# A fused encoder layer: 20 of its 24 token-tile transposes leave TensorE for VectorE blocks of 32 and a turn through DRAM

## Chip, cores and metric

The kernel runs on one core of one Trainium2 chip. The metric is device microseconds of one execution, median of the runs: 2145.7 us before (3 runs, 2145.51 to 2145.97).

## The reference

One encoder layer for two sequences, `x_prompt` (1024 tokens, below "the long sequence") and `x_sample` (512 tokens), each with 1024 features, in float32. Cut to what matters here:

```python
xn = _rmsnorm(x, norm_mix_g)
x  = x + _token_mixer(xn, w_in, ...)       # z = xn @ w_in, two attentions, gates, @ w_out
hn = _rmsnorm(x, norm_mlp_g)
x  = x + jnp.square(jax.nn.relu(hn @ w_up)) @ w_down
y  = _rmsnorm(x, norm_final_g)
```

Both `xn @ w_in` and `hn @ w_up` contract over the 1024 features, so on TensorE the normed activations must stand with features on the partitions: a normed tile of 128 tokens by 1024 features has to be turned into eight pieces of 128 features by 128 tokens.

## The kernel before, in words

All matmuls are in float32 by three products: each operand is split into a part `h` that ScalarE (ACT) copies out rounded, and a part `l`, the rest, that VectorE (DVE) subtracts; lines 195, 196 and 197 are the products h·h, l·h and h·l. So a turned tile is needed as `xs_…h` and `xs_…l` (for the token mixer) or as pieces of seven operands `B0`…`B6` (for the MLP, which is a seven-product scheme over two blocks of 768 tokens; `pair_t` makes the operands from two tiles, j and j+3 of a block, with sums and differences `ta1`…`ta4`).

The program is one long sequence. Trunk 0 mixes the 512 tokens of `x_sample` (4 tiles), trunk 1 the 1024 tokens of `x_prompt` (8 tiles), then comes the MLP over all 12 tiles. Every engine has its own instruction queue, filled in an order that a list scheduler fixed when the program was built, and each queue runs in that order: an instruction that waits holds up all behind it on its engine. SP (SyncE) only issues transfers, POOL (GpSimd) issues some too.

- **The switch from trunk 0 to trunk 1.** The last loop of a trunk is its out-projection, tile by tile (`ops` on TensorE, added to the residual `xrs` by DVE into `hs`). In trunk 0's second half of it, the normed MLP input `xnhs` of each tile is made and stored by POOL to a DRAM tensor `hnd` (L1215). Beside it, tiles 0 to 3 of the long sequence (`xas`, loaded at L1173) are normed into `xnns` and turned by `transpose_tile` (L282): eight TensorE transposes into PSUM `ptxs` (L290), an ACT copy to `xs_0h` (L300), a DVE subtraction to `xs_0l` (L306). Three are turned there, the fourth is carried into trunk 1, whose first loop multiplies tile by tile (`zs`, `zvs`) while it norms (`xts` to `xns`, L277) and turns tiles 4 to 7 the same way (into `xs_1h`, `xs_1l`). The norm's last step needs `rs_…`, a power that POOL works out (L180).
- **The end of trunk 1.** The same out-projection stores `xnhs` of trunk 1's first four tiles to `hnd`; its other four tiles are only added to `hd` (a DRAM tensor with the residual stream) and normed later, during the MLP (`late_norm`, store at L1558). SP fetches back the tiles of the first MLP block (`hn<-hnd`, L1099), and `pair_t` runs three times, each time with 16 TensorE transposes (L330) into PSUM `pt`, ACT copies to the operands (L339) and DVE differences (L342 to L358). Behind that SP loads `rawu`, the up weights, from which DVE makes the operands `A`; then TensorE starts the MLP's products `ua`, `ub`, `uc`, `ud`.
- **The second MLP block.** `hn_load` (L1277) fetches its six tiles from `hnd` and `pair_t` runs three times more, amid the last products of block one.

Of 24 transposed tiles the trace shows 12 at L290 (four of them `x_sample`'s) and 12 in pairs at L330. The buffers that matter: normed tiles and some `xrs` tiles share a pool tag `k4` of four buffers, fetched `hn` tiles share three.

Of the kernel before, what the change touches and what calls it, by code (L numbers as in the profile page):

```python
# [61 lines left out]
def encoder(ctx: ExitStack, tc: tile.TileContext, xs, outs, w):  # L62
# [19 lines left out]
    hnd = dram.tile([NTOK, D], F32, name="hnd")  # L82
# [198 lines left out]

    def transpose_tile(xn, dest, j, nm, pin=False, between=()):  # L282
# [42 lines left out]
    def pair_t(nm, j, tiles, B, banks, tmp):  # L325

        b11, b21, b12, b22 = banks
        for halves, t in (((b11, b21), tiles[0]), ((b12, b22), tiles[1])):
            for c in range(NC8):
                nc.tensor.transpose(  # L330
                    halves[c // 4][:, (c % 4) * P : (c % 4 + 1) * P], t[:, c * P : (c + 1) * P], ident
                )
# [11 lines left out]
        y1 = tmp(f"y1{nm}")  # L344
        a2, a1, a3, a4 = (tmp(f"ta{i}{nm}") for i in (2, 1, 3, 4))
        hi(0, b11)
        nc.scalar.activation(y1, b12, AF.Copy)

# [3 lines left out]
        nc.vector.tensor_tensor(a1, y1, b11, op=ALU.subtract)  # L352
        hi(2, a1)
        nc.vector.tensor_tensor(a2, b22, a1, op=ALU.subtract)
        nc.vector.tensor_tensor(a3, b22, y1, op=ALU.subtract)
# [11 lines left out]
    class Trunk:  # L367
# [15 lines left out]
        def p0_t(self, tt, xn, between=()):  # L383
# [3 lines left out]
            transpose_tile(xn, self.xhl[tb], j, f"x{self.N}_{tt}", self.t0 + tt < 3, between)  # L387
            self.ready = max(self.ready, tt + 1)
# [7 lines left out]
    def run(tr, nxt, first):  # L396
# [100 lines left out]
        for g in range(2):  # L497
            with phase(f"phR{N}_{g}") as ph:
                xn_of, pre = {}, {}
                fresh = g == 0 and tr.ready < NT  # L500
                if fresh and not first:
# [16 lines left out]
                    xt = norm_load(x, tr.ready, ph, f"{N}_{tr.ready}")  # L518
                    xn_next = ph.tile([P, D], F32, tag="xn", name=f"xn{N}_{tr.ready}", bufs=2)
# [61 lines left out]
                def next_norm(tt):  # L581
                    xn = ph.tile([P, D], F32, tag="xn", name=f"xn{N}_{tt}", bufs=2)
                    xn_of[tt] = norm_to(xn, norm_load(x, tt, ph, f"{N}_{tt}"), gb, f"{N}_{tt}")
# [74 lines left out]
                for tt in range(NT):  # L658
                    tb, j = divmod(tt, 4)
                    nm = f"{N}_{g}_{tt}"  # L660
                    def next_tile():
                        tr.p0_t(tt + 1, xn_of.pop(tt + 1))
                        if not first and tt + 3 < NT:
                            next_norm(tt + 3)
                        elif first and tt + 2 < NT:
# [5 lines left out]
                    to_come = fresh and tr.ready <= tt + 1 < NT  # L671
# [32 lines left out]
                    if fresh and not first:  # L704
                        if tt == 0:
                            tr.p0_t(*tr.carry.pop(0))
                        if tt == 1:
                            xn_of[tr.ready] = norm_to(xn_next, xt, gb, f"{N}_{tr.ready}")
                        if tt == 2:
                            next_norm(tr.ready + 1)  # L710
# [1085 lines left out]
```

## Time and profile before

| | |
|---|---|
| median of 3 runs | 2145.7 us |
| the profiled execution's span | 2144.2 us |
| TensorE (PE) busy | 2116.2 us, 99% |
| VectorE, ScalarE, GpSimd busy | 1462.7, 1146.2, 356.1 us |
| DMA, mean over the span | 165 GB/s; queue q1 (SP's) 277927 packets, 41.9% of 16 engines |

A row of the timeline reads: start, length (both us), engine, line, operation, output<-inputs, shapes; rows that follow each other are folded as xN, and what stands in brackets is the idle time before and what ended it. `SPq` is SP issuing; a DMA's time there is that of the issue, not of the data. Groups of instructions show busy time and the mean ns of one, then the idle time of the engine just before them. Matmuls are pipelined: their lengths overlap, so what one costs is seen by when the next one starts.

### The profile page before, as it was taken

Reading aid. Unit: us, or ns where it says so; the run is one execution under the profiler, and the core shown is the slowest. Engines: PE = TensorE matmul, PEld = TensorE weight load, DVE = VectorE, ACT = ScalarE, POOL = GpSimd, SP = SyncE. Lnnn points to the kernel's source line nnn. Section 1 sums busy time; section 2 is a strip of 40 time slices with the busy share of each in tenths; the row PEclk is TensorE's granted clock in tenths of the full one; section 3 lists DMA queues with packets and bytes.
Section 4 is the critical chain, followed back from the end, with each engine's and each line's share of the span. In section 5 each row is a group of like instructions: output and inputs, shape, how many; then the busy total and the mean of one; then the engine's idle time right before and its main releaser. Section 6 shows DMA issues by size and latency. Waiting matters only on the chain.

```text
span 2144.2 us, 32083 instructions
## 1 busy us (share of the span) xinstructions
PE 2116.2 (99%) x10967; PEld 1847.3 (86%) x10967; DVE 1462.7 (68%) x2793; ACT 1146.2 (53%) x2511; POOL 356.1 (17%) x446
## 2 busy tenths in 40 slices
PE   9999999999999999999999999999999999999998
PEld 8888778888897888887888899999999988888886
DVE  6665786767657755656882877777777777659563
ACT  6664653767566644555530566566655643434342
POOL 2232310323232223333200200003000000000000
PEclk9999999999999999999999999999999999999999
DMA  6437557520122133444472665578545799688561
GB/s 190 133 98 212 152 162 251 186 71 25 57 79 68 42 95 108 131 118 112 140 240 103 213 194 184 171 248 205 165 142 157 256 353 343 212 279 281 165 206 59
DMA packets 321259, 354.08 MB, mean 165 GB/s; under 512 B 31551, under 2 KB 255431, under 8 KB 321095
## 3 DMA queue, kind: packets, MB, share of 16 engines
q1 hardware_dynamic: 277927, 279.65, 41.9%
q10 hardware_dynamic: 36016, 52.19, 7.0%
q0 software_dynamic: 7152, 20.19, 3.5%
q8 instruction: 87, 1.43, 0.3%
q14 instruction: 77, 0.63, 0.1%
HBM read 264.85 MB, written 87.88 MB: 165 GB/s over the span
## 4 chain that ended last, share of the span: by engine, by line
PE 67%; DVE 1%; issue 1%; DMA 0%; ACT 0%; POOL 0%; SPq 0%; POOLq 0%; ACTq 0%; DVEq 0%
PE dn L195 6%; PE dn L196 6%; PE dn L197 6%; PE ua L195 2%; PE ua L196 2%; PE ua L197 2%; PE ud L195 2%; PE ud L196 2%; PE ud L197 2%; PE uc L195 2%; PE uc L196 2%; PE uc L197 2%; PE gpss L195 2%; PE gpss L197 2%; PE gpss L196 2%; PE ops L197 1%
## 5 line engine op out<-in xcount | busy, mean ns | idle before, releaser
L197 PE MATMUL dn<-wd,al 128*128 128x512 f32 x624 | 242.8, 389 | 0.0
L196 PE MATMUL dn<-wd,ah 128*128 128x512 f32 x624 | 242.8, 389 | 0.0
L195 PE MATMUL dn<-wd,ah 128*128 128x512 f32 x624 | 242.7, 389 | 0.0
L1273 ACT ACTIVATE ah<-ar 128x512 fp32r<-128x512 f32 x168 | 104.4, 628 | 203.1 <-PE dn L196 177.1
L1274 DVE TENSOR_TENSOR al<-ar,ah 128x512 fp32r<-128x512 f32 x168 | 113.9, 685 | 71.6 <-ACT ah L1273 64.0
L197 PEld LDWEIGHTS dn<-wd,al 128*128 128x128 f32 x624 | 117.1, 188 | 24.4
L195 PEld LDWEIGHTS dn<-wd,ah 128*128 128x128 f32 x624 | 117.1, 188 | 24.3
L196 PEld LDWEIGHTS dn<-wd,ah 128*128 128x128 f32 x624 | 117.1, 188 | 24.2
L749 POOL TENSOR_SCALAR ps<-ps,rls 128x1024 f32<-128x1024 f32 (+1 forms) x96 | 96.8, 1010 | 225.7 <-DVE rls L748 200.4
L788 ACT ACTIVATE pths<-pTs 128x512 fp32r<-128x512 f32 x160 | 94.0, 597 | 74.0 <-PE pTs L783 71.9
L789 DVE TENSOR_TENSOR ptls<-pTs,pths 128x512 fp32r<-128x512 f32 x160 | 107.6, 686 | 37.7 <-ACT pths L788 36.9
L743 DVE TENSOR_REDUCE nms<-ss 128x1 f32<-128x1024 f32 (+1 forms) x96 | 99.8, 1040 | 25.6 <-PE ss L741 25.0
L195 PE MATMUL gpss<-xs_0h,w_gs 128*128 128x512 f32 x256 | 105.5, 412 | 0.5 <-DVE ot_Bs L440 0.4
L746 ACT ACTIVATE ps<-ss,nms 128x1024 f32<-128x1024 f32 (+1 forms) x96 | 93.2, 972 | 22.8 <-DVE nms L743 20.2
L783 PEld LDWEIGHTS pTs<-ident,ps 128*128 128x128 f32 x640 | 77.9, 140 | 28.5 <-POOL ps L749 4.3
L180 POOL TENSOR_TENSOR rs_f<-ms_f,mhalf 128x1 f32<-128x1 f32 x6 | 4.0, 667 | 590.7 <-DVE ms_f L176 590.7
L197 PE MATMUL gpss<-xs_0h,w_gs 128*128 128x512 f32 x256 | 101.1, 395 | 0.2 <-DVE w_gs L190 0.2
L196 PE MATMUL gpss<-xs_0l,w_gs 128*128 128x512 f32 x256 | 101.0, 394 | 0.0
L783 PE MATMUL pTs<-ident,ps 128*128 128x128 f32 x640 | 99.0, 274 | 1.3 <-DVE ptls L789 0.6
L1273 ACT ACTIVATE A<-S 128x512 fp32r<-128x512 f32 x128 | 75.9, 623 | 31.5 <-DVE S L1336 22.7
L957 POOL TENSOR_TENSOR bms<-rects,msks 128x384 f32<-128x384 f32 (+1 forms) x72 | 70.1, 977 | 129.1 <-DVE nmbs L974 107.6
L1392 ACT ACTIVATE c<-c 128x384 f32<-128x384 f32 x96 | 50.3, 524 | 69.4 <-DVE c L1391 69.3
(330 smaller groups left out, 6419.7 us busy)
## 6 DMA issues: line engine op xcount, KB each, us to landing
ar<-ud SPq DMA_DIRECT2D x120, 512.0 KB, 5.3
br<-in_w_mlp_down_dram SPq DMA_DIRECT2D x72, 512.0 KB, 5.2
rawu<-in_w_mlp_up_dram SPq DMA_DIRECT2D x64, 512.0 KB, 4.1
ud<-c ACTq DMA_DIRECT2D x128, 192.0 KB, 3.2
raw_gs<-in_w_in_dram SPq DMA_DIRECT2D x32, 512.0 KB, 4.0
zgs<-sgs ACTq DMA_DIRECT2D x48, 256.0 KB, 2.2
ud<-cs SPq DMA_DIRECT2D x64, 192.0 KB
raw_os<-in_w_out_dram SPq DMA_DIRECT2D x16, 512.0 KB, 3.9
```

What stands on the lines that cost most here:

```text
L195: nc.tensor.matmul(out, ah, bh, start=start, stop=False, **kw)
L196: nc.tensor.matmul(out, ah, bl, start=False, stop=False, **kw)
L197: nc.tensor.matmul(out, al, bh, start=False, stop=stop, **kw)
L743: nc.vector.tensor_reduce(nm_, s, axis=AX.X, op=ALU.max, negate=True)
L746: nc.scalar.activation(p, s, AF.Exp, bias=nm_, accum_out=l)
L749: nc.gpsimd.tensor_scalar(p, p, rl, 1.0, op0=ALU.mult, op1=ALU.mult)
L783: nc.tensor.transpose(pt[:, j * P : (j + 1) * P], PP[u, j][:, kc * P : (kc + 1) * P], ident)
L788: nc.scalar.activation(hi, pt, AF.Copy)
L789: nc.vector.tensor_tensor(lo, pt, hi.bitcast(F32), op=ALU.subtract)
L957: nc.gpsimd.tensor_tensor(bm.rearrange("p (r c) -> p r c", c=32), rects[h][:, ir : ir + kr_n, jr : jr + 32], msk[:, hf * 3 + ct, :].rearra ...
L1273: nc.scalar.activation(hi, src, AF.Copy)
L1274: nc.vector.tensor_tensor(lo, src, hi.bitcast(F32), op=ALU.subtract)
```

## The change

For trunk 1's eight tiles and the MLP's twelve, the TensorE transposes go. In their place `send_t` transposes a normed tile where it lies, in blocks of 32 by 32 (DVE, one instruction of 128x1024), and writes it to a DRAM tensor that has features as rows (`xt` for trunk 1, `hnt` in place of `hnd`) by four transfers of 32x32x32 elements, each of 1024 runs of 128 bytes: 20 transposes, 80 transfers. Trunk 1's writes are issued by SP, the MLP's by POOL. A trunk-1 tile is then fetched back by two SP transfers (128x4x128, runs of 512 bytes) straight into its `xs_…l` buffers, and `split` makes h by an ACT copy and l by a DVE subtraction in place. The MLP's tiles are fetched as before by one SP transfer each, now from `hnt` in runs of 512 bytes instead of 4 KB, and `pair_t` reads them from SBUF instead of PSUM; the copy `y1` goes, as it only kept one of its inputs out of PSUM. `x_sample`'s own four tiles are turned by TensorE as before.

```diff
+    def send_t(dst, col, t, eng):
+        v = t.rearrange("p (b i) -> p b i", i=32)
+        nc.vector.transpose(v, v)
+        rows_of = dst.rearrange("(b i) t -> i b t", i=32)
+        for a in range(4):
+            eng.dma_start(rows_of[:, :, col + 32 * a : col + 32 * a + 32], v[32 * a : 32 * a + 32])
+
+    def hn_fetch(raw, t0):
+        nc.sync.dma_start(
+            raw.rearrange("p (c t) -> p c t", t=P), hnt.rearrange("(c p) t -> p c t", p=P)[:, :, t0 : t0 + P]
+        )
...
-    def pair_t(nm, j, tiles, B, banks, tmp):
-        b11, b21, b12, b22 = banks
-        for halves, t in (((b11, b21), tiles[0]), ((b12, b22), tiles[1])):
-            for c in range(NC8):
-                nc.tensor.transpose(
-                    halves[c // 4][:, (c % 4) * P : (c % 4 + 1) * P], t[:, c * P : (c + 1) * P], ident
-                )
+    def pair_t(nm, j, tiles, B, tmp):
+        b11, b21, b12, b22 = (t[:, q * 512 : q * 512 + 512] for t in tiles for q in range(2))
...
+        def send(self, tt, xn):
...
+            send_t(self.xt, tt * P, xn, nc.sync)
+            for q in range(2):
+                nc.sync.dma_start(
+                    self.xhl[tb][1][q][:, :, js].bitcast(F32),
+                    self.xt[q * 512 : q * 512 + 512, tt * P : (tt + 1) * P].rearrange("(c p) t -> p c t", p=P),
+                )
+        def split(self, tt):
...
+            for hi, lo in parts:
+                nc.scalar.activation(hi, lo.bitcast(F32), AF.Copy)
+            for hi, lo in parts:
+                nc.vector.tensor_tensor(lo, lo.bitcast(F32), hi.bitcast(F32), op=ALU.subtract)
...
-                    xn_of[tt] = norm_to(xn, norm_load(x, tt, ph, f"{N}_{tt}"), gb, f"{N}_{tt}")
+                    tr.send(tt, norm_to(xn, norm_load(x, tt, ph, f"{N}_{tt}"), gb, f"{N}_{tt}"))
...
-                    while ahead:
-                        nxt.p0_t(*ahead.pop(0))
+                    while len(ahead) > 1:
+                        nxt.split(ahead.pop(0))
...
-                            nc.gpsimd.dma_start(hnd[rows_, :], hn)
+                            send_t(hnt, r0, hn, nc.gpsimd)
```

The order of the queues moves with it. At the switch, SP's queue stood as follows before (names end in the tile's number and a running number; `xas` and `xts` are input tiles, `raw_…` weights, `rts` rope tables):

```order
L478 DMA rawkvs1_0_4695<-in_w_in_dram 128x8x64 x2
L1173 DMA xas0_1_1_4474<-in_x_prompt_dram 128x1024
L1173 DMA xas0_1_2_4539<-in_x_prompt_dram 128x1024
L223 DMA raw_vs1_0_0_4704<-in_w_in_dram 128x4x256
L223 DMA raw_vs1_0_4_4709<-in_w_in_dram 128x4x256
L1173 DMA xas0_1_3_4600<-in_x_prompt_dram 128x1024
L223 DMA raw_gs1_2304_0_0_5390<-in_w_in_dram 128x8x128
L109 DMA gbs1_4674<-in_norm_mix_g_dram 128x1024
```

In the changed kernel the same stretch of SP's queue holds the writes (L288, into the turned tensor `xts1_4480`) and the fetches (L405) of tiles 0 to 2; those of tile 3 follow behind it, ahead of `gbs1`:

```order
L1207 DMA xas0_1_1_4490<-in_x_prompt_dram 128x1024
L288 DMA xts1_4480<-xnns0_1_0_4468 32x32x32 x4
L405 DMA xs1_0l0_4478<-xts1_4480 128x4x128
L405 DMA xs1_0l1_4479<-xts1_4480 128x4x128
L1207 DMA xas0_1_2_4549<-in_x_prompt_dram 128x1024
L223 DMA raw_vs1_0_0_4718<-in_w_in_dram 128x4x256
L223 DMA raw_vs1_0_4_4723<-in_w_in_dram 128x4x256
L223 DMA raw_gs1_2304_0_0_5391<-in_w_in_dram 128x8x128
L288 DMA xts1_4480<-xnns0_1_1_4532 32x32x32 x4
L288 DMA xts1_4480<-xnns0_1_2_4595 32x32x32
L405 DMA xs1_0l0_4478<-xts1_4480 128x4x128
L405 DMA xs1_0l1_4479<-xts1_4480 128x4x128
```

A fetch can be issued only when its tile's four writes have landed, and on SP the next tile's loads and writes stand behind it; tile 1's fetch also stands behind the first write of tile 2.

DVE's queue at the same place, before: the l part of tile 0 (`xs1_0l`, L306), the norm of tile 1 (`xnns0_1_1`), the l parts of the projection weights `wgls`, then tile 1's l part:

```order
L306 TENSOR_TENSOR xs1_0l0_4503<-ptxs1_0_4505,xs1_0h0_4501 128x4x128
L306 TENSOR_TENSOR xs1_0l1_4504<-ptxs1_0_4505,xs1_0h1_4502 128x4x128
L266 SCALAR_TENSOR_TENSOR xnns0_1_1_4529<-xas0_1_1_4474,rs_ns0_1_1_4534,gns0_4288 128x1024
L1199 TENSOR_TENSOR hs0_1_4285<-ops0_1_2_4541,xrs0_1_2_4537 128x512
L190 TENSOR_TENSOR wgls1_0_0_4682<-rawqs1_0_0_4683,wghs1_0_0_4681 128x2x256 x2
L190 TENSOR_TENSOR wgls1_0_1_4686<-rawqs1_0_1_4687,wghs1_0_1_4685 128x2x256 x2
L306 TENSOR_TENSOR xs1_0l0_4503<-ptxs1_1_4566,xs1_0h0_4501 128x4x128
```

And in the changed kernel (L418 is the l part in `split`, L285 the transpose):

```order
L285 STREAM_TRANSPOSE xnns0_1_0_4468<-xnns0_1_0_4468 128x1024
...
L418 TENSOR_TENSOR xs1_0l0_4478<-xs1_0l0_4478,xs1_0h0_4476 128x4x128
L418 TENSOR_TENSOR xs1_0l1_4479<-xs1_0l1_4479,xs1_0h1_4477 128x4x128
L190 TENSOR_TENSOR wgls1_0_0_4696<-rawqs1_0_0_4697,wghs1_0_0_4695 128x2x256 x2
...
L190 TENSOR_TENSOR wgls1_0_1_4700<-rawkvs1_0_4709,wghs1_0_1_4699 128x2x128 x2
L266 SCALAR_TENSOR_TENSOR xnns0_1_1_4532<-xas0_1_1_4490,rs_ns0_1_1_4537,gns0_4288 128x1024
L285 STREAM_TRANSPOSE xnns0_1_1_4532<-xnns0_1_1_4532 128x1024
...
L285 STREAM_TRANSPOSE xnns0_1_2_4595<-xnns0_1_2_4595 128x1024
L418 TENSOR_TENSOR xs1_0l0_4478<-xs1_0l0_4478,xs1_0h0_4476 128x4x128
```

The l part of tile 0 now stands ahead of all of `wgls` and of tile 1's norm and transpose; tile 3's norm likewise stands behind tile 2's l part, tile 4's behind tile 3's, tile 7's behind tile 5's.

At the end of trunk 1, SP's queue before, from the fetch of the second pair of MLP tiles on (`hn0_1` and `hn0_4` are that pair, `hn0_2` and `hn0_5` the third):

```order
L1099 DMA hn0_4_13264<-hnd_87 128x1024
L1166 DMA xrs1_1_4_13266<-in_x_prompt_dram 128x512
L1099 DMA hn0_2_13337<-hnd_87 128x1024
L1166 DMA xrs1_1_5_13341<-in_x_prompt_dram 128x512
L1166 DMA xrs1_1_6_13415<-in_x_prompt_dram 128x512
L1166 DMA xrs1_1_7_13444<-in_x_prompt_dram 128x512
L1099 DMA hn0_5_13339<-hnd_87 128x1024
L1309 DMA rawu0_0_0_13515<-in_w_mlp_up_dram 128x4x256
```

And now:

```order
L1200 DMA xrs1_1_4_13263<-in_x_prompt_dram 128x512
L1200 DMA xrs1_1_5_13318<-in_x_prompt_dram 128x512
L1200 DMA xrs1_1_6_13372<-in_x_prompt_dram 128x512
L1200 DMA xrs1_1_7_13401<-in_x_prompt_dram 128x512
L291 DMA hn0_4_13261<-hnt_87 128x8x128
L291 DMA hn0_2_13314<-hnt_87 128x8x128
L291 DMA hn0_5_13316<-hnt_87 128x8x128
L1339 DMA rawu0_0_0_13472<-in_w_mlp_up_dram 128x4x256
```

The four residual loads `xrs` take buffers of the tag `k4` over from normed tiles, so each waits until POOL's four writes of one tile have landed (the last of them: until POOL's addition of `xrs1_1_4` to `hd`); the fetches `hn0_4`, `hn0_2`, `hn0_5` and the weights `rawu` now all stand behind them.

63 lines of the change are left out of this document (35 added, 28 removed).

## The prediction, on record before the changed kernel ran

> **What bounds the kernel.** First the head of the page, with the engines' busy time, and the chain that ended last:
>
> ```profile
> span 2144.2 us, 32083 instructions
> ...
> PE 2116.2 (99%) x10967; PEld 1847.3 (86%) x10967; DVE 1462.7 (68%) x2793; ACT 1146.2 (53%) x2511; POOL 356.1 (17%) x446
> ...
> PE 67%; DVE 1%; issue 1%; DMA 0%; ACT 0%; POOL 0%; SPq 0%; POOLq 0%; ACTq 0%; DVEq 0%
> ```
>
> TensorE sets the end: all its idle time is 2144.2 − 2116.2 = 28 us. A transpose taken off TensorE therefore counts in full, as long as its replacement arrives in time; and whatever makes TensorE wait counts in full too. The profiled execution's span is 1.5 us under the median of 2145.7; I sum against the span and add 1.5.
>
> **What is removed.** A transpose's own length (273 ns) overlaps its neighbours', so I read its price from the starts, in the timeline of TensorE, once at L290 and once at L330:
>
> ```profile
> 368.58 1.03 PE L290 MATMUL ptxs<-ident,xnns 128*128 128x128 f32 x8
> 369.37 0.47 PE L197 MATMUL ops<-wh_os,mgs 128*128 128x512 f32 x1
> ...
> 1177.08 1.91 PE L330 MATMUL pt<-ident,hn 128*128 128x128 f32 x16
> 1178.75 0.48 PE L195 MATMUL ops<-wh_os,mgs 128*128 128x512 f32 x1
> ```
>
> Eight cost 369.37 − 368.58 = 0.79 us, sixteen 1.67 us. Eight groups of eight and six of sixteen: 8 × 0.79 + 6 × 1.67 = 16.3 us. That is all that can be gained; 160 × 273 ns would be 43.7 us and is wrong.
>
> **What replaces them: one round trip.** The rows for its parts (groups by line, DMA issues with their landing, packets in a window with only small writes):
>
> ```profile
> L266 DVE SCALAR_TENSOR_TENSOR xnns<-xas,rs_ns,gns 128x1024 f32<-128x1024 f32 x3 | 3.8, 1282 | 0.3 <-POOL rs_ns L180 0.2
> L1484 DVE TENSOR_TENSOR br<-br,br 128x1024 f32<-128x1024 f32 x16 | 19.5, 1218 | 1.6 <-DMA br<-in_w_mlp_down_dram 1.6
> ```
>
> ```profile
> L306 DVE TENSOR_TENSOR xs_0l<-ptxs,xs_0h x16: 678/682/692, 10.0 to 393.7; 128x512 fp32r<-128x512 f32 x16
> ...
> L300 ACT ACTIVATE xs_0h<-ptxs x16: 578/596/600, 9.4 to 391.9; 128x512 fp32r<-128x512 f32 x16
> ...
> L169 SPq DMA_DIRECT2D shifted<-pad x16: 323/406/1537, 18.8 to 35.0; - x16
> ```
>
> ```profile
> q1 hardware_dynamic: 1065, 0.23, 27.3%
> ```
>
> ```profile
> x23s<-in_x_sample_dram SPq DMA_DIRECT2D x2, 512.0 KB, 7.3
> ...
> raw_pas<-in_w_proj_a_dram SPq DMA_DIRECT2D x16, 256.0 KB, 4.2
> ...
> hd<-xrs POOLq DMA_DIRECT2D x4, 256.0 KB, 3.8
> hd<-hs SPq DMA_DIRECT2D x4, 256.0 KB, 2.0
> ```
>
> The transpose of 128x1024 is not in the trace; the simple DVE rows of that shape take 1.22 to 1.28 us, a third of it to twice it are my bounds (0.4 to 2.5), and I take 1.2. A write has 1024 runs of 128 bytes. The nearest row is `shifted<-pad` (runs of 192 bytes; the window 30 to 34 us holds 1065 packets, mostly its own): 0.273 × 16 × 4 us / 1065 = 16.4 ns a packet, so 1024 packets on 16 engines take 1.05 us. Issue 0.41 us, landing 2.0 us after it (`hd<-hs`). The trip, from the end of the transpose: four issues 1.6, last landing 2.0, two fetch issues 0.8, landing 4.2 (`raw_pas`, the same 256 KB in runs of 512 bytes), first h part 0.6, two l parts 1.3: **10.5 us**. Its lower bound is 8.3 (the fetch lands in 2.0, as `hd<-hs`), its upper 16 (7.3 as `x23s`, and 2.4 more for four writes of 1.05 us queued one behind another). Before, the same way took 0.8 + 1.1 + 1.3 us on TensorE, ACT and DVE.
>
> The table in the Trainium skill's VectorE: DVE Perf Modes, section "The three transpose paths", has TensorE at 390 ns and VectorE at 311 ns per 128×128 (in bf16, VectorE only in 32×32 blocks), and its rules for kernel authors keep TensorE where PSUM will do. By its figure, an estimate, a tile's eight pieces take 2.5 us on DVE instead of my 1.2, and the five transposes that stand in the chain below would add some 6 us; no run here shows it yet, and TensorE's 0.79 us for eight, in the row above, is well below its 390 ns each.
>
> **The switch, place one.** DVE's and SP's orders chain the trips. The start is fixed by DVE's norm of tile 0, and TensorE's end by its tile products:
>
> ```profile
> 367.12 1.28 DVE L266 SCALAR_TENSOR_TENSOR xnns<-xas,rs_ns,gns 128x1024 f32<-128x1024 f32 x1
> ...
> 371.82 1.29 DVE L306 TENSOR_TENSOR xs_0l<-ptxs,xs_0h 128x512 fp32r<-128x512 f32 x2
> ...
> 375.10 2.48 DVE L190 TENSOR_TENSOR wgls<-rawqs,wghs 128x512 fp32r<-128x512 f32 x4
> ...
> 381.50 1.09 DVE L190 TENSOR_TENSOR wgls<-rawkvs,wghs 128x256 fp32r<-128x256 f32 x3
> ```
>
> ```profile
> 379.00 0.51 PE L195 MATMUL zs<-wghs,xs_0h 128*128 128x384 f32 x2
> ...
> 397.24 0.34 PE L195 MATMUL zs<-wghs,xs_0h 128*128 128x384 f32 x1
> ...
> 407.05 0.42 PE L195 MATMUL zs<-wghs,xs_1h 128*128 128x384 f32 x1
> ...
> 408.93 0.44 PE L197 MATMUL zs<-wghs,xs_1l 128*128 128x384 f32 x1 [1.29 <-DVE xs_1l L306]
> ...
> 433.48 0.42 PE L195 MATMUL zs<-wghs,xs_1h 128*128 128x384 f32 x1
> ```
>
> Tile 0 is normed and transposed by 370. Its l part is done at 380.5 (before: 373). All of `wgls` follows it (2.5 + 1.5 us): 384.5, so the first tile's products finish about 3 us late. Tile 1's norm and transpose: 387. Its fetch stands on SP behind the first write of tile 2, whose two norms and two transposes (5 us) end at 392: fetch issued at 392.4, l part at 399. Tile 2's other writes and fetch follow: 403.3. Tile 3's norm and transpose wait for that: 405.8; its trip ends at 416.3, where its products began at 397.24 before. Tile 4's norm stands behind that and some rope work (2.5 us): transposed at 421.3; its fetch waits on SP for tile 5's first write: products from 433, where they began at 407.05. From there TensorE itself is the limit: tiles 4 to 7 took 433.48 − 407.05 = 26.4 us, less three groups of transposes (2.4) and the 1.3 us wait: 22.7, so tile 7 begins at 455.7 instead of 433.48; tile 7's own trip (norm behind tile 5's l part, 440 + 10.5) ends earlier. That is **+22 us**. All eight groups of eight lie before this point and are in the difference already.
>
> POOL adds to it: its power for tile 1's norm stands behind the four MLP writes of one tile, tile 3's behind those of another.
>
> ```profile
> L1215 POOL DMA_DIRECT2D hnd<-xnhs x8: 576/576/582, 365.7 to 1181.7; - x8
> ...
> 186.85 0.56 POOL L941 DMA_DIRECT2D kBs<-kBs  x1 [9.02 <-DVE rlbs L981]
> ...
> 801.41 0.60 POOL L941 DMA_DIRECT2D kBs<-kBs  x1 [10.82 <-DVE kBs L937]
> ```
>
> One POOL transfer of 128 runs takes 0.576 us; no row has 1024 runs. Bounds: 0.58 (runs cost nothing) and 4.6 (eight times as much). `kBs` has 64 runs in trunk 0 and 128 in trunk 1, 0.56 and 0.60 us: 0.6 ns a run, some 0.6 us for 896 more; a little above that I take **1.3 us**, 5.2 a tile, by those rows. That puts tile 1's norm where it stands already, and tile 3's some 3 us later: **+25 us** for the switch. At 0.58 it is 22; at 4.6, 18.4 us a tile, tile 3's norm would come 35 us later.
>
> The Trainium skill, DMA: Bandwidth & Descriptors, "Anatomy of one DMA — SWDGE (gpsimd) path", says that many descriptors can be emitted before the incremental cost shows. By it the lower end of 0.58 holds and the whole sum is some 6 us less; the two `kBs` lengths speak for a small but visible cost.
>
> **The end of trunk 1, place two.** TensorE, SP, POOL and DVE rows:
>
> ```profile
> 1207.16 0.45 PE L195 MATMUL ub<-B,A 128*128 128x384 f32 x1 [0.72 <-ACT A L1273]
> ```
>
> ```profile
> 1178.48 0.42 SPq L1099 DMA_DIRECT2D hn<-hnd  x1
> ...
> 1188.67 0.38 SPq L1099 DMA_DIRECT2D hn<-hnd  x1
> 1189.15 25.55 SPq L1309 DMA_DIRECT2D rawu<-in_w_mlp_up_dram  x7
> ```
>
> ```profile
> 1177.28 0.69 DVE L1199 TENSOR_TENSOR hs<-ops,xrs 128x512 f32<-128x512 f32 x1 [1.36 <-PE ops L197]
> ...
> 1188.97 0.69 DVE L342 TENSOR_TENSOR B<-pt,B 128x512 fp32r<-128x512 f32 x1 [0.76 <-ACT B L339]
> ...
> 1195.53 0.69 DVE L342 TENSOR_TENSOR B<-pt,B 128x512 fp32r<-128x512 f32 x1
> ```
>
> A pair takes DVE 1195.53 − 1188.97 = 6.6 us, and before, pairs 1 and 2 began at 1189 and 1195.5. Now DVE's order puts the norms and transposes of tiles 1 and 2 (5 us) behind the add of tile 3 (1177.3): done by 1183, POOL's eight writes of them by 1193.5, landed 1195.5. The load of the fifth residual tile waits for the first four of them, the sixth for the rest, the seventh for POOL's addition behind them (issued near 1193, landing 3.8): about 1196.5. Only then `hn0_4`, issued at about 1178.5 before. It lands near 1201.5; pair 1 ends at 1208; `hn0_5` needs a buffer that pair 1 frees, so it lands near 1211.5, and pair 2 ends at 1218. Then the last residual add and `A`'s first parts (0.7 + 4 × 0.65 + 0.6): `ub` at about 1222 instead of 1207.16: **+15 us**, the six groups before it included. Bounds: −5 (the waits are all covered and three pairs' transposes saved) and +30 (two late landings of 7.3 us).
>
> **Place three, the second block.** Its three pairs have no transposes left: −5.0 us. DVE works nearly without a pause there:
>
> ```profile
> 1437.00:1441.50 4.50, 4.50 (x34) 4.43 (x32) 4.47 (x9) 2.96 (x6) 0.00 (x0) 1.00 0.72 241
> ```
>
> 4.47 of 4.5 us busy: a pair's DVE work is no shorter, and its fetched tiles are now held until DVE has read them. I count **−3**, between −5 and +3. The four late norms store at 1248.7 to 1336.0, and the second block's loads run from 1417.5 (rows below): four POOL writes each and a transpose lie in 80 us of slack, and cost nothing.
>
> ```profile
> L1282 SPq DMA_DIRECT2D hn<-hnd x6: 319/332/410, 1417.5 to 1455.1; - x6
> L1558 POOL DMA_DIRECT2D hnd<-xnl x4: 576/576/582, 1248.7 to 1336.0; - x4
> ```
>
> **Sum:** +25 + 15 − 3 = +37; 2144.2 + 37 + 1.5 = **2183 us**. Lower ends: trips of 8.3 us take 2.2 off each of four (25 − 9 = 16), −5, −5: +6, 2152. Upper ends: trips of 16 (25 + 22), +30, +3: +80, 2226.
>
> **Rivals.**
> (a) Faster: the round trips are hidden. If a trip takes about 4 us (writes and fetches that overlap what stands between them), tile 3's products start on time and `hn0_4` early enough; then only the 16.3 us count: 2129. It decides at the point where trip plus queue at tile 3 stays below 397.2 − 373; for it speaks that DVE is 68% busy and DMA not full; against it that two landings in a row alone have 2.0 + 4.2 us in the rows.
> (b) Slower, by POOL: 4.6 us a write. The switch +25 + 35, the trunk's end +15 + 2 × 13, −3: +98, 2244. For it: nothing in the trace has so many runs; against it: the two `kBs` lengths.
> (c) The end of trunk 1 is covered by its products and only the switch counts, with trips of 8.3 us: +16 − 5 − 5 = +6 to +16, about 2155 to 2162.
>
> **Chances:** forecast 0.5, (a) 0.12, (b) 0.13, (c) 0.22, near no change 0.03. The range 2148 to 2240 takes in (c), the forecast's ends and part of (b). Faster by over 0.2% (4.3 us, about what a measurement of this kernel can tell) 0.12, same 0.03, slower 0.85.
>
> **What would show it.** TensorE's largest waits become those for l parts at L418 (tiles 3 and 4 above all), with products of tile 3 near 416 to 419 and of tile 7 near 456 to 459; SP has long stretches between L288 and L405; `ub` begins some 15 us later against the end of the `ops` products; L285 near 1.2 us; POOL's L288 near 1.3. Wrong would be: no waits at L418, a landing under 1 us, or POOL at 4.6 us.

## The result, and the profile after

| | before | after |
|---|---|---|
| median of five runs, us | 2145.7 | 2220.8 |
| lowest to highest | 2144.97 to 2146.36 | 2216.56 to 2222.53 |
| span of the profiled execution, us | 2144.2 | 2220.2 |

The ratio is 1.0346, 95% interval [1.0333, 1.0359]: 75 us slower. The forecast was 2183 us, slower too, but 38 us too few. The head of the page after:

```profile
span 2220.2 us, 31911 instructions
...
PE 2122.8 (96%) x10807; PEld 1849.9 (83%) x10807; DVE 1499.7 (68%) x2813; ACT 1148.0 (52%) x2505; POOL 391.9 (18%) x482
...
PEclk9999999779999999999999999999999999999999
...
PE 62%; DVE 3%; DMA 1%; issue 1%; ACT 1%; POOL 0%; ACTq 0%; SPq 0%; POOLq 0%; DVEq 0%
```

TensorE has 160 instructions less and is busy 6.6 us longer; its idle time went from 28 to 97 us, and the granted clock has two slices at 0.7, where it was full before. These slices (388 to 500 us) and most of the idle time belong to one place, the switch from trunk 0 to trunk 1. TensorE's waits name it (what waited, on whom, us in all, times, longest):

```profile
PE zs L195 <- ACT xs_0h L416: 16.0, 3, 11.2
PE zs L195 <- ACT xs_1h L416: 12.1, 4, 4.5
PE pqs L621 <- ACT rrs L685: 10.8, 3, 4.1
PE ub L195 <- ACT A L1303: 8.7, 1, 8.7
PE zs L195 <- ACT wghs L184: 8.4, 1, 8.4
PE ua L195 <- ACT B L347: 5.6, 1, 5.6
PE ua L196 <- DVE B L350: 5.1, 1, 5.1
PE zs L197 <- DVE xs_1l L418: 4.5, 4, 2.6
```

Five rows are of the tile products of trunk 1 and their heads, 51.8 us; the three with `ua` and `ub`, 19.4 us, are the end of trunk 1. The waits at the tile products are for h parts (L416, 28.1 us) far more than for l parts (L418, 4.5 us), which the prediction had named. In the timeline of TensorE, the first product of tiles 0, 3, 4 and 7, the first of the second half's output products, and the two places at the end of trunk 1:

```profile
384.71 0.69 PE L195 MATMUL zs<-wghs,xs_0h 128*128 128x384 f32 x1 [8.43 <-ACT wghs L184]
...
423.22 0.69 PE L195 MATMUL zs<-wghs,xs_0h 128*128 128x384 f32 x1 [4.39 <-ACT xs_0h L416]
...
448.54 0.69 PE L195 MATMUL zs<-wghs,xs_1h 128*128 128x384 f32 x1 [4.48 <-ACT xs_1h L416]
...
493.15 0.69 PE L195 MATMUL zs<-wghs,xs_1h 128*128 128x384 f32 x1 [1.67 <-ACT xs_1h L416]
...
1172.32 0.39 PE L195 MATMUL ops<-wh_os,mgs 128*128 128x512 f32 x1
...
1265.18 0.69 PE L195 MATMUL ua<-B,A 128*128 128x384 f32 x1 [5.63 <-ACT B L347]
...
1283.42 0.69 PE L195 MATMUL ub<-B,A 128*128 128x384 f32 x1 [8.71 <-ACT A L1303]
```

Before, tile 7 began at 433.48, that output product (row below) at 1111.76, `ub` at 1207.16:

```profile
1111.76 0.39 PE L195 MATMUL ops<-wh_os,mgs 128*128 128x512 f32 x1
```

So the three terms of the sum measure **+60.6 at the switch** (1172.32 − 1111.76), **+15.7 at the end of trunk 1** (1283.42 − 1207.16 = 76.3, less 60.6) and **−0.3 behind it** (76.0 of span, less 76.3). Predicted were +25, +15 and −3.

The durations that had to be bounded, now measured (groups by line with min/median/max in ns, median landing, and one stretch of SP's queue: the four writes of tile 0):

```profile
L285 DVE STREAM_TRANSPOSE xnns<-xnns x4: 1235/1245/1246, 367.8 to 413.9; 128x1024 f32<-128x1024 f32 x4
...
L288 POOL DMA_DIRECT2D hnt<-xnhs x32: 786/786/855, 366.4 to 1258.1; - x32
L288 SPq DMA_DIRECT2D xts<-xnns x16: 303/614/2267, 369.0 to 416.8; - x16
```

```profile
xts<-xnns SPq DMA_DIRECT2D x16, 128.0 KB, 3.9
xs_0l<-xts SPq DMA_DIRECT2D x8, 256.0 KB, 3.2
```

```profile
369.02 4.92 SPq L288 DMA_DIRECT2D xts<-xnns  x4
```

The transpose is 1.24 us (1.2 taken; not the 2.5 of the other estimate). A POOL write of 1024 runs is 0.79 us (1.3 taken); rival (b) is out. In the median, a write lands after 3.9 us (2.0 taken), a fetch after 3.2 (4.2 taken). One step was priced from a row that didn't fit: an SP write of 1024 runs takes 0.6 us of SP in the median and up to 2.3, so tile 0's four took 4.9 us, not 1.6. From the end of the transpose to the end of the l parts, with all that stood ahead in the queues, tiles 0 to 3 took 14.9, 14.3, 15.2 and 9.5 us; 10.5 was taken for a trip with nothing ahead of it. How much of the landings is owed to the other transfers there (the DMA engines were busy for 0.57 to 0.89 of each 10 us between 380 and 450 us) no run separates.

### The profile page after: what moved, and what is told of

Its sections match the earlier page's. It is cut to its first block, busy times and chain, and to the rows that moved or that the text cites. A ratio compares the mean times of both kernels' runs of the same rounds, so it can differ in the third digit from the quotient of the medians.

```text
span 2220.2 us, 31911 instructions
## 1 busy us (share of the span) xinstructions
PE 2122.8 (96%) x10807; PEld 1849.9 (83%) x10807; DVE 1499.7 (68%) x2813; ACT 1148.0 (52%) x2505; POOL 391.9 (18%) x482
## 4 chain that ended last, share of the span: by engine, by line
PE 62%; DVE 3%; DMA 1%; issue 1%; ACT 1%; POOL 0%; ACTq 0%; SPq 0%; POOLq 0%; DVEq 0%
PE dn L195 6%; PE dn L197 6%; PE dn L196 6%; PE ua L197 2%; PE ud L195 2%; PE ud L196 2%; PE ua L196 2%; PE ud L197 2%; PE ua L195 2%; PE gpss L195 2%; PE gpss L197 2%; PE uc L196 2%; PE uc L195 2%; PE gpss L196 2%; PE uc L197 2%; PE pTs L817 1%
## 5 line engine op out<-in xcount | busy, mean ns | idle before, releaser
L195 PE MATMUL ua<-B,A 128*128 128x384 f32 x256 | 86.5, 338 | 5.6 <-ACT B L347 5.6
```

The costliest lines, as they stand in the source:

```text
L195: nc.tensor.matmul(out, ah, bh, start=start, stop=False, **kw)
```

## The experiments

Each ran on a chip together with the kernel before, whose medians there were 2145.3 to 2145.7. Intervals are of the ratio to those runs. Where a run is called the changed kernel with something, it is to be set against 2220.8. Further on, "run 2" means the runs of section 2. The code is cut to what changes; `NoSync` stands for the full argument that makes a dependency one of order alone. The order of the queues is fixed anew for each kernel, so an edit can move it elsewhere too: in the second run of section 1 tile 1 is normed at 373.2, ahead of tile 0's l part, and in the changed kernel at 387.9, behind it.

### 1. The MLP's tiles alone, and the long sequence's tiles alone

The first is the kernel before with `send_t`, `hn_fetch` and the new `pair_t` for the MLP's tiles; trunk 1's tiles stay on TensorE. The second is the rest.

```diff
-    nc.gpsimd.dma_start(hnd[rows_, :], hn)      # the first
+    send_t(hnt, r0, hn, nc.gpsimd)
...
-    ahead.append((tt, norm_tile(xt, gn, ph, f"n{nm}", "k4", 4)))      # the second
+    nxt.send(tt, norm_tile(xt, gn, ph, f"n{nm}", "k4", 4))
+    ahead.append(tt)
```

> Only the MLP's twelve tiles go through VectorE and DRAM; the long sequence's eight are turned on TensorE as before. If the two places simply add (my account: in the changed kernel the second half of trunk 0's out-projection to that of trunk 1's took 60.6 us longer, the stretch from there to the first ub 15.7, the rest 1.4 less): 2145.7 + 14, about 2160 us, with products of tile 7 near 434 us as before. Rival: POOL's four writes a tile hold up its powers at the switch, and a good part of the 60 us stays without the long sequence's trips: over 2170, with waits for rs there.

> Only the long sequence's tiles go through VectorE and DRAM; the MLP's are stored and turned as before. If the switch's loss is that of the trips: 2145.7 + 60, about 2206 us, and the end of trunk 1 as before. Rival, POOL's MLP writes are part of the loss at the switch: 2190 or less.

Measured: the MLP's tiles alone 2171.2 us, 1.0118 [1.0103, 1.0133], +25.5; trunk 1's alone 2194.5 us, 1.0223 [1.0207, 1.0238], +48.8. The first has its rival's time, but there VectorE waits no more than 0.7 us at a time for POOL's powers; the second lies between its two expectations. Together 74.3, the whole 75.1: in total the two parts add up. By places, the MLP's tiles cost 8.7 us at the switch (output products from 1120.4), 15.0 at the end of trunk 1 and 1 behind it. The trunk's tiles cost 48.5, all at the switch; with the 8.7 that is 57.2 of the 60.6. The 8.7 us are nearly three times the 3 that the prediction gave to POOL there. POOL's time for the writes (3.2 us a tile) is not the whole of it: the load of tile 3's input takes over the buffer of a normed MLP tile and waits until that tile's writes have landed (waits of SP between 370 and 392, the run with the MLP's tiles alone):

```profile
SPq L1178 <- DMA hnt<-xnhs: 11.1, 2, 8.5
```

The load is issued at 389.1 instead of 378.2, and tile 3's norm starts at 395.5 instead of 388.9.

### 2. Tiles 4 to 7 alone, and tiles 0 to 3 alone

Half of the trunk's round trips each, with the MLP's tiles as before.

```diff
 def next_tile():   # only tiles 4 to 7
-    tr.p0_t(tt + 1, xn_of.pop(tt + 1))
+    tr.split(tt + 1)
...
-    xn_of[tt] = norm_to(xn, norm_load(x, tt, ph, f"{N}_{tt}"), gb, f"{N}_{tt}")
+    tr.send(tt, norm_to(xn, norm_load(x, tt, ph, f"{N}_{tt}"), gb, f"{N}_{tt}"))
```

> The kernel before, with only tiles 4 to 7 of the long sequence through VectorE and DRAM; tiles 0 to 3 and the MLP's tiles on TensorE. In the run with all eight tiles alone, the products of tile 3 began 15.9 us later than before and those of tile 7 another 32 us later. The prediction had TensorE as the limit between tiles 4 and 7. Theory: the trips of these tiles cost by themselves, since each tile's products, rope and the next norm wait for each other: +25 to +35, 2171 to 2181 us. Rival, the prediction's own: once tile 4 has come they follow at TensorE's pace, and only tile 4's first trip shows: +5 to +15, 2151 to 2161 us.

> The kernel before, with only tiles 0 to 3 of the long sequence through VectorE and DRAM; tiles 4 to 7 and the MLP's tiles on TensorE. Theory: the loss is that of the first four tiles in the run with all eight, +16 us, about 2162, as tiles 4 to 7 then need only TensorE. Rival: the loads behind tile 3's fetch on SP (gain row, tile 4's input, rope tables) carry the delay on: +25 us or more, 2171.

Measured: tiles 4 to 7 alone 2173.4 us, 1.0138 [1.0121, 1.0155], +28; tiles 0 to 3 alone 2163.2 us, 1.0084 [1.0069, 1.0099], +18. Together 46 of the 48.8; both as their theories had it. So the larger half lies where the prediction saw TensorE at its limit. The profiled execution of the first is 24.7 us over the kernel before: 7.2 of them are tile 4's own trip (407.05 before), and 17.4 arise between tile 4 and tile 7. With tiles 4 to 7 alone, tile 3 starts at 396.6 as before, but tile 4 at 414.3, tile 5 at 428.3, tile 6 at 440.7, tile 7 at 458.0. ScalarE's rows there show what the fetched tiles wait for:

```profile
426.34 0.38 ACT L650 ACTIVATE vts<-zvs 128x256 fp32r<-128x256 f32 x1 [5.89 <-PE zvs L197]
...
427.62 1.15 ACT L419 ACTIVATE xs_1h<-xs_1l 128x512 fp32r<-128x512 f32 x2
...
436.56 0.38 ACT L650 ACTIVATE vts<-zvs 128x256 fp32r<-128x256 f32 x1 [7.79 <-PE zvs L197]
...
437.88 1.06 ACT L273 ACTIVATE xns<-xts 128x1024 f32<-128x1024 f32 x1 [0.94 <-DVE vts L651]
...
440.02 1.18 ACT L419 ACTIVATE xs_1h<-xs_1l 128x512 fp32r<-128x512 f32 x2
```

Tile 5's fetch was issued at 417.0 and tile 6's at 423.5; their h copies run at 427.6 and 440.0, each behind a copy of `zvs` that waited 6 and 8 us for TensorE. And TensorE makes `zvs` behind the products of the tile before, which waited for its own h copy. Each tile so holds up the next. Tile 7's norm stands behind the same copy: its step on ScalarE (L273) runs only at 437.9, though its input was loaded from 421.1 on, and its four writes begin at 442.7.

### 3. The h copies ahead of the value copies

Tiles 4 to 7 alone again, with NoSync dependencies that put ScalarE's and VectorE's two `vts` operations behind the `split` of the tile that comes next.

```diff
+    if fresh and not first and 2 <= tt < 6:
+        for late, early_ in zip(v_op, tr.parts):
+            tc.add_manual_dep(late.ins, early_.ins.name, NoSync, reason="order")
```

> Only tiles 4 to 7 go through DRAM, as in the run that cost 28 us, but ScalarE's copies of a fetched tile into its h part, and VectorE's l parts, are pinned ahead of the vt copies (L650 there) that wait for TensorE's zv products. Theory (the in-order queues of ScalarE and VectorE, not the transfers, made tiles 5 to 7 late): tile 5's products start 3 to 4 us earlier than 428.3, tile 7's at 440 to 447 instead of 458.0, and the cost falls from 28 us to 10 to 16 us, a median of 2156 to 2162. Rival (the round trips themselves set the pace, the copies only stand where they would have waited anyway): tile 7's products stay within 3 us of 458 and the median at 2170 to 2176.

Measured: 2165.0 us, 1.0094 [1.008, 1.0108], +20 instead of +28. Neither range holds it. Tile 7 starts at 452.1 (458.0; 440 to 447 expected), so the order is part of the cause: 8 us of 28 by the medians, 5.6 of 24.7 between the two profiled executions. But tile 5 still starts at 429.1: another copy now stands ahead of its h copy, one that waits for the heads' transposes of an earlier tile:

```profile
427.44 0.28 ACT L629 ACTIVATE kTs<-pqs 128x128 fp32r<-128x128 f32 x1 [6.45 <-PE pqs L625]
...
428.39 1.15 ACT L419 ACTIVATE xs_1h<-xs_1l 128x512 fp32r<-128x512 f32 x2
```

The same kind of wait, one instruction further on. And ahead of tile 7's products, TensorE's own order has transposes of the heads, which wait 4.5 us for the rope work of an earlier tile (`pqs` at 449.49). What is left of the 20 us when no such copy stands ahead was not tried.

### 4. A warm TensorE

The changed kernel with 280 dummy transposes on TensorE in the waits of the tile products, so that its clock is full when a tile comes.

```diff
+WARM = {0: 48, 1: 88, 3: 40, 4: 40, 6: 40, 7: 24}
...
+    if fresh and not first and tt in WARM:
+        warm_up(WARM[tt], ...)
     z = mm(f"z{nm}")[:, :384]
```

> The changed kernel, with transposes of no use put on TensorE ahead of the products of tiles 0, 1, 3, 4, 6 and 7 of the long sequence, in the gaps where it waits (284 in all, about 0.1 us each at full clock). The trace after shows a granted clock of 0.5 to 0.85 between 380 and 500 us, and TensorE about 19 us longer busy there than its instructions take at full clock. Theory: that half-rate time lies on the chain (tile products, rope, the next norm), and a clock held up gives much of it back: 2202 to 2212 us. Rival: the trips set the pace and slow products only fill the waiting: within 5 us of 2220.8, although the clock is near 1.0.

Measured: 2229.0 us, 1.0381 [1.0364, 1.0399], 8 us slower than the changed kernel, outside both ranges. Its windows (length, then busy us and count of PE, PEld, DVE, ACT, POOL, then the granted clock, DMA share, GB/s):

```profile
390.00:400.00 10.00, 9.06 (x79) 8.79 (x77) 6.39 (x8) 2.19 (x4) 4.25 (x6) 1.00 0.97 209
...
420.00:430.00 10.00, 6.38 (x20) 5.88 (x20) 2.34 (x5) 2.82 (x8) 1.69 (x3) 0.66 0.73 229
```

Up to 400 the clock is full and tile 0's products run at full speed, yet tile 1 starts at 403.7, 0.3 us later than without dummies: there the trip sets the pace, not the clock. But tile 1's dummies were through 4.6 us before it came, and from 400 to 410 the clock was at 0.66 again, so tiles 2 and 3 (410.6 and 423.6, 0.5 and 0.4 us later) show nothing of it. Later dummies were in the way as well: 34 of them held tile 3's last products from 434.8 to 439.1. What a full clock would give in tiles 4 to 7 stays open.

### 5. Loads on another queue, norms ahead of the l parts

First, rope tables and input tiles of that loop on ScalarE's queue instead of SP's. Second, tile 0's and tile 2's l parts behind the transpose of the tile after, on VectorE.

```diff
-    op = nc.sync.dma_start(rt, w["rope"][tt * P : (tt + 1) * P])      # the first
+    op = (nc.sync if first else nc.scalar).dma_start(rt, w["rope"][tt * P : (tt + 1) * P])
...
     op = nc.vector.tensor_tensor(lo, lo.bitcast(F32), hi.bitcast(F32), op=ALU.subtract)      # the second
+    if tt in (0, 2):
+        tc.add_manual_dep(op.ins, self.turned[tt + 1].ins.name, NoSync, reason="order")
```

> The changed kernel, with the loads of the long sequence's tiles 4 to 7 and of its rope tables issued by ACT instead of SP in trunk 1, so that they no longer stand behind the fetches that wait on SP. In the trace after, rope tables were issued at 421.8, behind tile 3's fetch, and the norm of tile 4 ran at 433, behind the rope work that waited for them. Theory: SP's order is a term of its own; tile 4's norm some 8 us earlier, 2208 to 2213 us. Rival: ACT or the trips take it back: within 3 us of 2220.8.

> The changed kernel, with one edge more in DVE's order: the l parts of tiles 0 and 2 stand behind the norm and transpose of tiles 1 and 3, not ahead of them. The prediction's step was that these norms are late because they stand behind those l parts. Theory: tile 1 is transposed some 4 us earlier (POOL's power for it is ready at 383.5), tile 3 a little, and the tiles behind follow: 2212 to 2217 us. Rival: writes, fetches and POOL set the pace and DVE's order is no term of its own: within 3 us of 2220.8.

Measured: 2226.3 us, 1.0374 [1.0359, 1.039], and 2227.2 us, 1.038 [1.0364, 1.0395]: each about 6 us slower than the changed kernel, outside both of its ranges. In the first, tile 4's norm came 5 us earlier (427.7 for 433.0), but its fetch (L405) stood on SP behind the first write of tile 5, whose input now came late on the other queue; five of SP's writes took 13 us with what they waited for, and the fetch went out when it had in the changed kernel (443.75; timeline of SP):

```profile
430.60 13.06 SPq L288 DMA_DIRECT2D xts<-xns  x5
443.76 1.71 SPq L405 DMA_DIRECT2D xs_1l<-xts  x2
```

In the second, tile 1's norm was at 388.1 as ever: the `wgls` parts ahead of it waited for ScalarE's `wghs`, and these stand behind the h copies of tile 0, which wait for the fetch:

```profile
384.36 1.29 DVE L190 TENSOR_TENSOR wgls<-rawqs,wghs 128x512 fp32r<-128x512 f32 x2 [4.75 <-ACT wghs L184]
```

Both moved one wait and met the next one in another in-order queue.

### 6. The end of trunk 1: the residual loads, then the order of norms and writes

First, the residual inputs of the last four tiles in buffers of another tag (`zs`), so that their loads don't wait for normed tiles to be written. Second, the same with the adds pinned behind the norm and transpose of the tile before, and tile 4's write to `hd` behind tile 3's four writes.

```diff
-    xr = ph.tile([P, D], F32, tag="k4", name=f"xr{nm}", bufs=4)[:, 0:512]      # both
+    xr = tmp_zs(f"xr{nm}")
...
+    tc.add_manual_dep(add.ins, turn.ins.name, NoSync, reason="order")      # the second
+    tc.add_manual_dep(op.ins, sent.ins.name, NoSync, reason="order")
```

> The changed kernel, with the last four residual tiles of trunk 1 in buffers of the tag zs (their size) instead of k4, so that their loads wait for none of POOL's writes and SP reaches the fetch of hn0_4 early. The prediction's step: those waits hold up hn0_4, hn0_2, hn0_5 and rawu, and cost the 15.7 us measured from the start of that half of the out-projection to the first ub. Theory: 11 to 16 us come back, 2205 to 2210 us, hn0_4 issued some 15 us earlier. Rival: the late norms of tiles 1 and 2 on DVE and POOL's writes hold up hn0_5 all the same: less than 6 us come back.

> The changed kernel with the residual inputs of trunk 1's last four tiles in other buffers (the run that moved nothing), and four pins more at the end of trunk 1: the add of tile t+1 stands behind the norm and transpose of tile t on VectorE, tile 4's add behind tile 3's transpose, and tile 4's write to hd behind tile 3's four writes on GpSimd. Theory (order on VectorE and GpSimd keeps pair 0's tiles in their raw buffers, so that the fetch of tile 4 can't be issued): the fetch of hn0_4 is issued at 1241 to 1245 on the old run's clock instead of 1251.4, the stretch from the second half's first output products to the first up products falls from 108.1 to 98 to 102 us, and the median is 2211 to 2215. Rival (the buffers of the norms, or the transfers themselves, hold it): the stretch stays at 106 or more, the median at 2218 to 2222.

Measured: 2221.0 us, 1.0355 [1.034, 1.0371], and 2223.1 us, 1.0358 [1.0343, 1.0373]: nothing gained by either, much as both rivals had it. From the first of the second half's output products to `ub` the changed kernel takes 111.1 us, the first run 108.1, the second 111.3; before it was 95.4. The 3 us of the first run are lost again behind `ub` (940.3 us to the end instead of 936.8). No residual load waited for POOL's writes any more in either, and in the second the fetch of `hn0_4` was issued at 1246.9, in the first at 1251.4, and `ua` began at 1257.7, in the first at 1260.3. `ub` was not earlier (1281.9, in the first 1278.3): the last thing that it needs are the first up weights, `rawu`. Their load waits in SP's queue until DVE has read the last operand of a fetched tile (waits of SP between 1175 and 1300, first the changed kernel, then the kernel before):

```profile
SPq L1339 <- DVE ta L363: 8.3, 1, 8.3
```

```profile
SPq L1309 <- PE pt L330: 1.6, 1, 1.6
```

Before, TensorE's transposes freed those buffers. In the second run the loads that had waited were then issued within 3 us of each other, and the DMA engines were full for 11 us while TensorE stood still (windows of that run):

```profile
1268.00:1279.00 11.00, 0.00 (x0) 0.00 (x0) 2.17 (x3) 0.00 (x0) 2.39 (x5) 0.52 0.99 333
```

So what came earlier in the second run's chain was lost at its end. Buffers of their own for the fetched tiles were not tried.

### 7. The second block alone, and with GpSimd out of it

The kernel before, with only the MLP's second block changed; then the same with GpSimd's two l parts of each pair there on VectorE.

```diff
-    nc.gpsimd.dma_start(hnd[rows_, :], hn)      # both
+    if r0 < BT:
+        nc.gpsimd.dma_start(hnd[rows_, :], hn)
+    else:
+        send_t(hnt, r0, hn, nc.gpsimd)
...
-    lo(2, a1, nc.gpsimd)      # the second
-    lo(3, a3, nc.gpsimd)
+    lo(2, a1)
+    lo(3, a3)
```

> The kernel before, with only the MLP's second block changed: its six tiles are transposed by VectorE and fetched, and TensorE makes none of their 48 transposes; trunk 1's switch and the first block are as before. What the prediction said of this part: 3 us faster, 2142 to 2143. Theory from the changed kernel's profile (VectorE's subtractions on operands in SBUF take 1.2 us and more beside GpSimd's, instead of 0.68, and give the saving back): within 1.5 us of the kernel before, 2144 to 2147.

> As the run before it, with GpSimd's two l parts of each pair made by VectorE too in the second block, so that GpSimd does nothing beside them. Theory (the two engines slow each other down where both read SBUF): VectorE's ta operations of the second block's pairs fall to 0.68 to 0.75 us, its work in the block is about the same for six operations more, and the time is 1 to 3 us below the run before it. Rival (VectorE is simply in the way of the first products, whoever else works): the same or up to 3 us more than that run.

Measured: 2150.6 us, 1.0026 [1.0016, 1.0037], and 2150.2 us, 1.0021 [1.0012, 1.003]: 0.2 to 0.3% slower than the kernel before. The first is above both of its expectations; the second is not shown to differ from the first, as its rival had it. But the block itself is faster: from `ub` to the end the first takes 933.6 us against 937.0, −3.4, as predicted, and the second 934.5, −2.5. The loss is at the end of trunk 1 (from the first of the second half's output products to `ub` 102.4 us in both, 95.4 before): two of its tiles are written turned for this block, DVE's order there changed, and an add that waits for the load of the fifth residual tile stands ahead of tile 3's norm (timeline of VectorE, the first of the two):

```profile
1184.64 0.69 DVE L1254 TENSOR_TENSOR xrs<-ops,xrs 128x512 f32<-128x512 f32 x1 [6.43 <-DMA xrs<-in_x_prompt_dram]
```

The profiled executions are 2.3 and 4.0 us over the kernel before, the medians 5.2 and 4.8, so 1 to 3 us of the loss stand in no profile. Since the block itself is faster, the theory that DVE's slower operations eat the saving falls. They are slower beside GpSimd, and at their old speed without it (one of the `ta` operations, first run and second), and the time is the same as far as the runs tell (each scatters over more than 4 us):

```profile
L406 DVE TENSOR_TENSOR ta<-hn,ta x3: 677/1791/1793, 1451.1 to 1474.7; 128x512 f32<-128x512 f32 x3
```

```profile
L406 DVE TENSOR_TENSOR ta<-hn,ta x3: 684/684/684, 1453.2 to 1476.1; 128x512 f32<-128x512 f32 x3
```

## Why the prediction was right or wrong

**The removed transposes** and the argument that TensorE sets the end held: TensorE waits now, and its waits are what the change costs.

**The switch: the chain of trips right up to tile 3, what follows wrong, +25 for +60.6.** The chain of round trips came in the order that was foretold. By its own times (from tile 3 on with its 3 us for POOL):

| | predicted | measured |
|---|---|---|
| l part of tile 0 done | 380.5 | 383.9 |
| tile 1 transposed | 387 | 390.5 |
| l part of tile 2 done | 403.3 | 411.5 |
| tile 3's products begin | 419.3 | 423.2 |
| tile 4's products begin | 436 | 448.5 |
| tile 7's products begin | 458.7 | 493.2 |

At tile 0's l part it is 3.4 us late, most of it the four writes of tile 0 (4.9 us for 1.6), and at tile 2's 8.2. That tile 3 is only 4 us late is luck in part: it was transposed 6.4 us late (415.2 for 408.8), but its own trip took 8.0 us up to its products instead of 10.5. At tile 4 it is 12.5 us late. Here the prediction counted "some rope work" and left out what this work itself waits for: the rope tables are issued on SP behind tile 3's fetch, at 421.8, POOL's rope operation waits for a load until 429.7, and a rope operation of VectorE waits for POOL, ahead of tile 4's norm in its order. The load of tile 4's own input stands behind the same fetch (issued at 421.2, ScalarE waits for it until 429.2), so the norm could hardly have been earlier than 431 (timeline of VectorE after):

```profile
430.86 0.86 DVE L680 TENSOR_TENSOR ts<-ts,rts 128x320 f32<-128x320 f32 x1 [5.86 <-POOL us L673]
...
432.97 1.28 DVE L277 SCALAR_TENSOR_TENSOR xns<-xts,rs_s,gbs 128x1024 f32<-128x1024 f32 x1
```

From tile 4 to tile 7 it took 44.6 us, not 22.7, and this is the step that failed: "From there TensorE itself is the limit". Run 2 shows it alone: tiles 4 to 7 by themselves cost 28 us, and take 43.8 us from tile 4 to tile 7. In its place stands the loop of run 2: a fetched tile's h copy behind `vts` copies that wait for TensorE. It is in the changed kernel too, with the copy of tile 6 (L416) behind them:

```profile
460.51 0.38 ACT L647 ACTIVATE vts<-zvs 128x256 fp32r<-128x256 f32 x1 [5.59 <-PE zvs L197]
...
470.73 0.38 ACT L647 ACTIVATE vts<-zvs 128x256 fp32r<-128x256 f32 x1 [7.77 <-PE zvs L197]
...
474.19 1.18 ACT L416 ACTIVATE xs_1h<-xs_1l 128x512 fp32r<-128x512 f32 x2
```

Before, TensorE's transposes delivered a tile in the same stream as the products, so the order of ScalarE's queue fitted by itself; this is argued from the order, but in the rows before no `vts` copy between 395 and 435 waited more than 1.6 us. Run 3 shows the order to be worth 8 of the 28 us; how the rest divides among the trips, further copies and the clock is not settled.

**The clock was left out.** TensorE does the same products in more time, because the granted clock falls after its waits (windows after, and the sum of 380 to 440 before and of 380 to 500 after):

```profile
400.00:410.00 10.00, 6.36 (x24) 5.81 (x24) 4.10 (x6) 4.03 (x7) 1.72 (x3) 0.63 0.77 198
...
490.00:500.00 10.00, 7.45 (x23) 6.47 (x24) 5.08 (x11) 5.40 (x12) 0.00 (x0) 0.52 0.06 20
...
sum 120.00, PE 70.26 PEld 64.06 DVE 63.30 ACT 53.42 POOL 31.31; mean PE 5.85 PEld 5.34 DVE 5.27 ACT 4.45 POOL 2.61
```

```profile
sum 60.00, PE 57.27 PEld 55.23 DVE 41.94 ACT 40.20 POOL 22.33; mean PE 9.54 PEld 9.21 DVE 6.99 ACT 6.70 POOL 3.72
```

The stretch before includes six groups of transposes (4.7 us) and some 2 us of later work, so about 51 us of the same work became 70. Over the whole kernel TensorE is busy 6.6 us longer although 16.3 us of transposes are gone, so some 23 us are slow products. Not all of them count, since where a trip sets the pace a slow product is hidden (tile 1 in run 4).

**POOL** at the switch: the price of a write was too high (1.3 for 0.79 us), the term too low: 3 us for the 8.7 that the MLP's tiles cost there by themselves, because the load of tile 3's input, which waits for a normed tile's writes to land (run 1), was not counted. In the changed kernel that wait does not show: the load stands on SP behind the writes of tile 2 (issued at 403.3), and VectorE waits only 1.1 us for POOL's power at tile 3's norm. There the MLP's tiles are worth 12.1 us (60.6 less the 48.5 of run 1), with another order of VectorE's queue; how these come about stays open. The prediction's 6 us less for a write of 0.58 us are some 9 by its own rows (3 at the switch, eight writes of 0.72 us less at the end of trunk 1).

**The end of trunk 1: right in size, +15 for +15.7, and in its times, in part by luck.** Shifted by the 60.6 us, norms 1 and 2 were to be done by 1243.6 (1243.2 measured), `hn0_4` to be issued at 1257 (1256.6), `ub` at 1282.6 (1283.4). But POOL's eight writes were over at 1249.2, 5 us ahead of the foretold time, and the last residual load was out by 1254.1; `hn0_4` then waited 2.5 us more for a buffer that the first pair held, and at the end VectorE stood 3.3 us waiting for `rawu`, which the sum did not have. And the reason given, residual loads waiting for `k4` buffers, is not the whole: run 6 takes these waits away, and the way to `ub` is only 3 us shorter. Other waits stand beside it, those by VectorE's and GpSimd's order and by the release of the buffers for `rawu`; with one taken away, the next sets the end.

**The second block: −3 for −0.3, and right by itself.** Run 7 measures −3.4 and −2.5. In the changed kernel two waits are followed by slow products: at `ub` 14 of them start 0.32 us apart instead of 0.173 (1283.42 to 1287.87), some 2.1 us, and after a wait of 2.2 us, from 1554.35 to 1557.80, another 1.5 us. −3.4 + 2.1 + 1.5 = +0.2, or +1.1 from −2.5; this sum is argued from the rows, and no run isolates it.

**Rivals:** (a) falls by the landings, 3.9 us for a write and 3.2 for a fetch, and by trips of 9.5 us and more; (b) by 0.79 us a POOL write; (c) because the end of trunk 1 cost 12.7 to 15.9 us in every run with the first block's tiles through DRAM (and its lower time is 2152 by its own sum, not 2155).

## What to carry to other kernels

Work that leaves the engine which consumes it loses the place that it had in that engine's order: what was delivered in the stream of the products must now pass SP's, ScalarE's and VectorE's queues, each in its own order, and a wait in one stands ahead of what the others need. Count for each moved step what else stands in those queues, tile by tile to the last one, before calling the first engine the limit again; and count slow products after long new waits. Here 16 us of transposes were saved, and TensorE got 69 us more of waits and some 23 us of slow products: 76 us lost.

## What the hardware showed that was not expected

**Half rate after a wait.** Tile 4's products after their waits (TensorE after):

```profile
454.75 0.52 PE L195 MATMUL zs<-wghs,xs_1h 128*128 128x384 f32 x1
455.06 0.41 PE L196 MATMUL zs<-wgls,xs_1h 128*128 128x384 f32 x1
455.31 0.34 PE L197 MATMUL zs<-wghs,xs_1l 128*128 128x384 f32 x1
455.48 0.34 PE L195 MATMUL zs<-wghs,xs_1h 128*128 128x384 f32 x1
```

They start 0.32 us apart for 2.7 us (from 452.34), then 0.17 us; at `ub` it lasted 4.4 us, at tile 3 4.7 us (from 423.22). The Trainium skill, TensorE: Matmul & The Clock Gate, "Part 1: The HAM clock gate", has TensorE at half rate after an idle window and at full rate after some 3.4 us of sustained work: the trace agrees, with 2.7 to 4.7 us. No single idle time decides here: after the wait of 2.2 us that ended at 1552.81 the products went on 0.17 us apart for 1.5 us and only then turned slow, while in run 7 waits of 2.6 and 2.2 us at the same place were followed by no slow product (granted clock 1.00 from 1480 to 1490). It bears on this case as a price for the long waits that the change adds.

**VectorE beside GpSimd.** With both operands in SBUF, a VectorE subtraction of 0.68 us took 1.8 and up to 2.4 us while GpSimd's subtractions ran (which took 1.6 to 1.9 us instead of 1.29), and 0.68 without them (run 7). In the kernel before, with one operand in PSUM, none of these took over 0.7 us beside GpSimd. The Trainium skill, SBUF — State Buffer, "SBUF: two separate sides", says that the two share a pair of ports which one holds for a whole instruction, a VectorE operation with two SBUF inputs included; the rows of run 7 agree, and there the time did not change.

**Writes in runs of 128 bytes.** On SP one of 1024 runs holds the queue 0.3 to 2.3 us, the next ones waiting behind the first (four of tile 0 took 4.9 us); on POOL 0.79 us, against 0.58 for one of 128 runs.
